# Attention's scores in another PSUM ring, and three stages of attention and retention run at later steps

## The chip, the cores and the metric

The kernel runs on one core of a Trainium2 chip, as one launch. The metric is the device time of that core in microseconds. Engines are named as in the profile: PE is TensorE's matmul (PEld its weight loads), DVE is VectorE, ACT is ScalarE, POOL is GpSimd, SP is SyncE, which here only issues DMAs.

## The reference, cut to what matters

A block of an encoder over 256 tokens of width 2048, all in float32: a half-step SwiGLU feed-forward, then two token mixers side by side, then a second half-step feed-forward and a final RMSNorm. The mixers are what the change is about:

```
q_a, k_a, v_a, q_r, k_r, v_r, g_r, gate_a, gate_r = split(rmsnorm(x) @ w_in)
att = softmax(q_a k_a^T / sqrt(128) + bias, chunk-causal) v_a             # 8 heads of 128
ret = (decay * (rotary(q_r) rotary(k_r)^T)) v_r                            # 8 heads of 128
ret = silu(g_r) * ret * rsqrt(mean(ret^2) + eps)                           # per head
x = x + (sigmoid(gate_a) * (att @ w_out_att) + sigmoid(gate_r) * (ret @ w_out_ret)) @ w_out
```

With 256 tokens there are four chunks of 64. The kernel computes retention without the recurrent state, as masked scores over all 256 tokens with the decay as a table.

## The kernel before, in words

All big products are matmuls of a 128x128 block of activations with a 128x512 block of weights. Each operand is split in a high and a low float32r part, and a product is three matmuls: high by high, low by high, high by low (`three`, L147, L148, L150). The work is a list of steps, written out in advance. A standard step takes two 128-row blocks of weights, 512 columns and both 128-token blocks: 12 matmuls. For it a weight tile is loaded by SP's queue, ACT casts it to its high part (L136) and DVE subtracts to get the low part (L137). There are four pairs of tiles for the split weights.

The order on every engine is the order in which the program is written. Step c does this:

```python
prep_upto(c + min(SPLIT_BUFS, AHEAD[0] + c // AHEAD[1]) if c else 2)
for fn in due.pop(c, []):
    fn()
steps[c].products()
state["slots"] += 1
```

So it first splits the weights of step c+3 (the fourth pair becomes free with step c-1), then runs what is due at c in the order in which it was entered with `later(n, fn)` (n steps from now), then issues its matmuls. What follows the last step of a product (its `done`) is issued behind that step's matmuls.

Entries of this list are counted here from `mixed`, the first step of the retention's queries. Entries 0 to 31 are the projections QR0, KR0, QR1, KR1 (8 entries each; 0 and 1 are halves of four heads). Entries 32 to 47 multiply the attention's result by `w_out_att`, four column blocks of 4 entries, 48 to 63 the retention's by `w_out_ret`; entry 48+j of the first block reads heads 2j and 2j+1, and the same holds for 32+j. At the end of each of the attention's blocks DVE multiplies the gate into both token blocks (`siga`, L1148).

PSUM has eight banks in three rings: `acc` and `z` of three banks each, `side` of two. A standard product holds one bank of `acc` (first token block) and one of `z` (second) for its entries. `side` serves everything short: transposes, scores, values.

Attention's head h (L952 on) is five stages at entries HEAD_AT[h] + 0, 1, 2, 4 and 6, with HEAD_AT = 3, 6, 10, 13, 17, 20, 24, 27. `scores`: two matmuls into `as` (L962, L963), DVE scales and adds the bias (L970). `powers`: ACT's exponentials. `shares`: DVE divides by the sums (L992). `transposes`: three into `apt` (L998), ACT copies them out (L1000). `values`: matmuls into `av` (L1006, L1007), then `split_out`: ACT casts to `atth` (L388), DVE subtracts to `attl` (L389).

Retention's half b is entered when its keys are done (half 0 at entry 15, half 1 at entry 31), with wait = RET_WAIT[b] = 14 and 5. Head i's `scores` (into `rs`, L1031, L1032; DVE multiplies the decay in, `rp`, L1034, L1035) run at wait + 2i, its `values` (into `ro`, one bank of `acc` and one of `z` for all four heads, L1044 to L1046) at wait + 2i + 3. `finish`, at wait + 9, squares on ACT (L1054), sums on DVE (L1056), takes the power on POOL (L385), and multiplies norm and gate in on DVE (L1062). Three entries later `ret.put` transposes both token blocks of the half, eight transposes into two tiles of the side ring (`retp`, L394), and splits them into `reth` and `retl` (L388, L389), which the products with `w_out_ret` read.

The rotated queries and keys are transposed as well (`qr0p`, `kr0p`, `qr1p`, `kr1p`, L394), at entries 10, 11, 18, 19, 26, 27, 34, 35, each entered behind the stages of attention.

Of the kernel before, what the change touches and what calls it, by code (L numbers as in the profile page):

```python
# [38 lines left out]
HALF_K = D // P // 2  # L39
LEAD = (10, 8)  # L40
MIX_LEAD = 6
RET_WAIT = (14, 5)
HELD = 6
MIX_ADDED = (0,)
MIX_AHEAD = 12
# [37 lines left out]
def block_kernel(ctx: ExitStack, tc: tile.TileContext, x, g1, w1g, w1u, w1d, gm, w_in, rel, woa, wor, wo,  # L83
# [12 lines left out]
    def act_tile(dt, name):  # L96
        return apool.tile([P, 4, SEQ], dt, tag="act", name=name)

    def acc_tile(name, tag="acc"):
        return psum.tile([P, NB], F32, tag=tag, name=name, bufs=3)  # L100

    def side_tile(name):
        return psum.tile([P, NB], F32, tag="side", name=name, bufs=2)

    def tmp_tile(name, tag="t", bufs=None):
        return tmp.tile([P, NB], F32, tag=tag, name=name, bufs=bufs)
# [9 lines left out]
    def later(n, fn):  # L116
        due.setdefault(state["step"] + n, []).append(fn)
# [263 lines left out]
    def rsqrt(dst, ssum, n, width):  # L381

        v = small.tile([P, width], F32, tag="v", name="v")
        nc.vector.tensor_scalar(v, ssum, 1.0 / n, EPS, op0=ALU.mult, op1=ALU.add)
        nc.gpsimd.tensor_tensor(dst, v, mhalf[:, :width], op=ALU.pow)  # L385

    def split_out(ps, hi, lo):
        nc.scalar.copy(hi, ps)  # L388
        nc.vector.tensor_sub(lo, ps, hi.bitcast(F32))  # L389
# [564 lines left out]
    def attention(h):  # L954
        b, i = h // 4, h % 4
        hs = slice(i * HD, (i + 1) * HD)
        sm = {}

        def scores():
            q, k = tposed["qa", b], tposed["ka", b]  # L960
            ps = side_tile(f"as{h}")
            nc.tensor.matmul(ps[:, 0:SEQ], q[:, i, P:SEQ], k[:, i, :], start=True, stop=True)  # L962
            nc.tensor.matmul(ps[:, SEQ : SEQ + P], q[:, i, 0:P], k[:, i, 0:P], start=True, stop=True)  # L963
            room = act_tile(F32, f"p{h}").rearrange("p a q -> p (a q)")
            s = room[:, : 3 * P].rearrange("p (j k) -> p j k", j=3)
            sm["room"] = room
            p3 = ps[:, : 3 * P].rearrange("p (j k) -> p j k", j=3)

            for j, bj in ((0, 1), (1, 0), (2, 0)):
                nc.vector.scalar_tensor_tensor(  # L970
                    s[:, j, :], p3[:, j, :], scale, table["bias", b][:, i, bj * P : (bj + 1) * P], op0=ALU.mult, op1=ALU.add
                )
            m = small.tile([P, NT], F32, tag="m", name="m")
            tot = small.tile([P, NT], F32, tag="l", name="l")
            for t, js in ((1, slice(0, 2)), (0, slice(2, 3))):
                nc.vector.reduce_max(m[:, t : t + 1], s[:, js, :], axis=AX.XY)
            nc.vector.tensor_scalar_mul(m, m, -1.0)
            sm["p"], sm["m"], sm["tot"] = s, m, tot


        def powers():
            s, m, tot = sm["p"], sm["m"], sm["tot"]
            for t, js in ((1, slice(0, 2)), (0, slice(2, 3))):
                nc.scalar.activation(
                    s[:, js, :], s[:, js, :], AF.Exp, bias=m[:, t : t + 1], accum_out=tot[:, t : t + 1]
                )

        def shares():
            s, tot = sm["p"], sm["tot"]
            nc.vector.reciprocal(tot, tot)  # L990
            for t, js in ((1, slice(0, 2)), (0, slice(2, 3))):
                nc.vector.tensor_scalar_mul(s[:, js, :], s[:, js, :], tot[:, t : t + 1])  # L992

        def transposes():
            ps = side_tile(f"apt{h}")

            for j, c in ((2, 0), (0, 1), (1, 2)):
                nc.tensor.transpose(ps[:, c * P : (c + 1) * P], sm["p"][:, j, :], id_sb)  # L998
            pt = sm.pop("room")[:, 3 * P : 6 * P]
            nc.scalar.copy(pt, ps[:, : 3 * P])  # L1000
            sm["pt"] = pt

        def values():
            v = nat["va", b]
            ps = side_tile(f"av{h}")
            nc.tensor.matmul(ps[:, :SEQ], v[:, 0, hs], sm["pt"][:, :SEQ], start=True, stop=False)  # L1006
            nc.tensor.matmul(ps[:, P:SEQ], v[:, 1, hs], sm["pt"][:, SEQ:], start=False, stop=True)  # L1007
            hi, lo = att.alloc(b)
            split_out(ps[:, :SEQ], hi[:, i, :], lo[:, i, :])

        return (0, scores), (1, powers), (2, shares), (4, transposes), (6, values)

    def all_attention():
        for h in range(HEADS):
            for s, stage in attention(h):
                later(HEAD_AT[h] + s, stage)

    def retention(b):

        wait = RET_WAIT[b]  # L1020
        outs = {}

        def head(i):
            h = 4 * b + i
            hs = slice(i * HD, (i + 1) * HD)
            sm = {}

            def scores():
                q, k = tposed["qr", b], tposed["kr", b]
                ps = side_tile(f"rs{h}")  # L1030
                nc.tensor.matmul(ps[:, 0:SEQ], k[:, i, 0:P], q[:, i, :], start=True, stop=True)  # L1031
                nc.tensor.matmul(ps[:, SEQ : SEQ + P], k[:, i, P:SEQ], q[:, i, P:SEQ], start=True, stop=True)  # L1032
                s = act_tile(F32, f"rp{h}").rearrange("p a q -> p (a q)")[:, : 3 * P]
                nc.vector.tensor_mul(s[:, :SEQ], ps[:, :SEQ], table["decay", b][:, i, :])  # L1034
                nc.vector.tensor_mul(s[:, SEQ:], ps[:, SEQ : SEQ + P], table["decay", b][:, i, 0:P])  # L1035
                sm["s"] = s

            def values():
                if i == 0:
                    for t in range(NT):  # L1040
                        outs[t] = acc_tile(f"ro{b}{t}", ("acc", "z")[t])
                v = nat["vr", b]
                s = sm["s"]
                nc.tensor.matmul(outs[0][:, hs], s[:, 0:P], v[:, 0, hs], start=True, stop=True)  # L1044
                nc.tensor.matmul(outs[1][:, hs], s[:, P:SEQ], v[:, 0, hs], start=True, stop=False)
                nc.tensor.matmul(outs[1][:, hs], s[:, SEQ:], v[:, 1, hs], start=False, stop=True)  # L1046

            return scores, values

        def finish():  # L1050
            srcs = []
            for t in range(NT):
                sq = tmp_tile(f"rsq{b}{t}", "gate", 2)
                nc.scalar.activation(sq, outs[t], AF.Square)  # L1054
                ms = small.tile([P, 4], F32, tag="ms", name="ms")
                nc.vector.reduce_sum(ms, sq.rearrange("p (h d) -> p h d", h=4), axis=AX.X)  # L1056
                rs = small.tile([P, 4], F32, tag="rs", name="rs")
                rsqrt(rs, ms, HD, 4)
                o = tmp_tile(f"rg{b}{t}", "qk", 4)
                for i in range(4):  # L1060
                    hs = slice(i * HD, (i + 1) * HD)
                    nc.vector.scalar_tensor_tensor(  # L1062
                        o[:, hs], outs[t][:, hs], rs[:, i : i + 1], nat["gr", b][:, t, hs], op0=ALU.mult, op1=ALU.mult
                    )
                srcs.append(o)
            later(3, lambda: [ret.put(b, t, srcs[t]) for t in range(NT)])

        for i in range(4):
            for s, stage in enumerate(head(i)):
                later(wait + 2 * i + 3 * s, stage)  # L1070
        later(wait + 2 * 4 + 1, finish)

    w_in0 = w_in[0]

# [50 lines left out]
    for b in range(2):  # L1125
        add([proj(QR + b * NB, ret_qk_done("qr", b)), proj(KR + b * NB, ret_qk_done("kr", b, lambda b=b: retention(b)))])
# [209 lines left out]
```

## Time and profile before

| what | value |
|---|---|
| runs, median (lowest to highest) | 2048.49 us (2047.64 to 2049.56), 3 runs |
| profiled execution, its own time | 2048.31 us |
| its span, first to last instruction | 2046.5 us |
| PE busy, share of the span | 2031.7 us, 99% |
| PEld, DVE, ACT, POOL busy | 1678.3, 1788.5, 1499.2, 344.8 us |
| granted clock of PE, mean | 0.999 of full speed |

The busy share of PE counts overlapping matmuls as one stretch, so a matmul that starts 0.2 us later than it could is not seen in it; the start times in a timeline tell that. The attention and retention stages lie between 1060 and 1240 us of the span. A row of a timeline is: start in us, us until the last of the group ended, engine, line, operation, output<-inputs, shapes, count, and in brackets the idle time before it with what ended it.

### The profile page before, as it was taken

What the parts mean: (1) busy time and instruction counts of PE and PEld (TensorE: products, weight loads), DVE (VectorE), ACT (ScalarE), POOL (GpSimd) and SP (SyncE); (2) the same over time, 40 slices, a digit from 0 to 9 for tenths busy, and PEclk for the clock granted to TensorE, in tenths of its full rate; (3) what the DMA queues carried; (4) which work ended last, traced back from release to release, by engine and by line L of the source; (5) the groups of instructions that cost most, each with busy time, mean ns of one, the idle gap of its engine ahead of it and who ended that gap; (6) DMA issues with size and microseconds to landing.
All of it is one profiled execution on the core that took longest, in us unless ns stands there. A gap on an engine that the chain in (4) does not pass through costs nothing.

```text
span 2046.5 us, 26320 instructions
## 1 busy us (share of the span) xinstructions
PE 2031.7 (99%) x9188; PEld 1678.3 (82%) x9188; DVE 1788.5 (87%) x1837; ACT 1499.2 (73%) x1890; POOL 344.8 (17%) x403
## 2 busy tenths in 40 slices
PE   9999999999999999999999999999999999999998
PEld 7788888888888878888888888888788888888886
DVE  7999999999998799999987667569989999989996
ACT  7788887878887777777775434556788788888785
POOL 1221122212113021211120000011112221112200
PEclk9999999999999999999999999999999999999999
DMA  8888899988878689899896645576889988889973
GB/s 289 249 248 259 254 269 278 265 242 246 264 231 264 234 228 310 272 281 286 254 321 221 212 148 197 187 240 180 269 262 269 278 248 234 267 257 268 278 206 134
DMA packets 226853, 506.33 MB, mean 247 GB/s; under 512 B 15824, under 2 KB 16576, under 8 KB 226720
## 3 DMA queue, kind: packets, MB, share of 16 engines
q1 hardware_dynamic: 154560, 297.31, 43.1%
q0 software_dynamic: 67952, 198.36, 37.1%
q10 hardware_dynamic: 4208, 8.99, 1.2%
q8 instruction: 72, 1.18, 0.2%
q14 instruction: 61, 0.50, 0.1%
HBM read 472.08 MB, written 12.06 MB: 237 GB/s over the span
## 4 chain that ended last, share of the span: by engine, by line
PE 94%; DVE 2%; DMA 2%; issue 1%; ACT 0%; POOL 0%; DVEq 0%; POOLq 0%; ACTq 0%
PE acc L150 15%; PE acc L147 15%; PE acc L148 15%; DMA z1030k<-in_ffn_w_up_dram 1%; DMA z1030x<-z1030k 1%; DVE lo L137 0%; DMA raw<-in_ffn_w_gate_dram 0%; PE z704a L150 0%; PE z425a L147 0%; PE z922a L147 0%; PE z885a L148 0%; PE z226a L147 0%; PE z190a L147 0%; PE z46a L147 0%; PE z262a L148 0%
## 5 line engine op out<-in xcount | busy, mean ns | idle before, releaser
L137 DVE TENSOR_TENSOR lo<-raw,hi 128x1024 fp32r<-128x1024 f32 x351 | 428.6, 1223 | 117.7 <-ACT hi L136 116.1
L136 ACT CAST hi<-raw 128x1024 fp32r<-128x1024 f32 x351 | 367.9, 1051 | 178.7 <-PE acc L148 133.4
L824 ACT ACTIVATE xall<-acc 128x512 f32<-128x512 f32 x160 | 94.5, 590 | 13.5 <-PE acc L150 9.7
L821 ACT ACTIVATE acc<-xall 128x512 f32<-128x512 f32 x160 | 95.9, 600 | 2.5
L147 PE MATMUL acc<-hi,mgh 128*128 128x512 f32 x128 | 50.2, 392 | 0.0
L148 PE MATMUL acc<-hi,mgl 128*128 128x512 f32 x128 | 49.8, 389 | 0.0
L150 PE MATMUL acc<-lo,mgh 128*128 128x512 f32 x128 | 35.5, 389 | 0.0
L147 PE MATMUL acc<-hi,nma01h 128*128 128x512 f32 x80 | 32.5, 407 | 0.0
L147 PE MATMUL acc<-hi,nma00h 128*128 128x512 f32 x80 | 32.3, 404 | 0.0
L148 PE MATMUL acc<-hi,nma01l 128*128 128x512 f32 x80 | 31.3, 391 | 0.0
L148 PE MATMUL acc<-hi,nma00l 128*128 128x512 f32 x80 | 31.2, 390 | 0.0
L148 PE MATMUL acc<-hi,nma11l 128*128 128x512 f32 x80 | 31.2, 390 | 0.0
L147 PE MATMUL acc<-hi,nma11h 128*128 128x512 f32 x80 | 31.2, 390 | 0.0
L147 PE MATMUL acc<-hi,nma10h 128*128 128x512 f32 x80 | 31.2, 390 | 0.0
L148 PE MATMUL acc<-hi,nma10l 128*128 128x512 f32 x80 | 31.2, 390 | 0.0
L150 PEld LDWEIGHTS acc<-lo,mgh 128*128 128x128 f32 x128 | 24.0, 188 | 5.0
L148 PEld LDWEIGHTS acc<-hi,mgl 128*128 128x128 f32 x128 | 24.0, 188 | 4.9
L147 PEld LDWEIGHTS acc<-hi,mgh 128*128 128x128 f32 x128 | 24.0, 188 | 4.9
L147 PE MATMUL acc<-hi,atth 128*128 128x512 f32 x64 | 26.2, 410 | 0.0
L147 PE MATMUL acc<-hi,reth 128*128 128x512 f32 x64 | 25.3, 395 | 0.0
L148 PE MATMUL acc<-hi,attl 128*128 128x512 f32 x64 | 25.1, 392 | 0.0
L148 PE MATMUL acc<-hi,retl 128*128 128x512 f32 x64 | 24.9, 389 | 0.0
(6884 smaller groups left out, 7265.9 us busy)
## 6 DMA issues: line engine op xcount, KB each, us to landing
raw<-in_ffn_w_down_dram SPq DMA_DIRECT2D x176, 512.0 KB, 6.8
raw<-in_w_in_dram SPq DMA_DIRECT2D x80, 512.0 KB, 5.2
raw<-in_w_out_dram SPq DMA_DIRECT2D x32, 512.0 KB, 3.7
raw<-in_ffn_w_up_dram SPq DMA_DIRECT2D x16, 512.0 KB, 4.6
raw<-in_w_out_att_dram SPq DMA_DIRECT2D x16, 512.0 KB, 4.2
raw<-in_w_out_ret_dram SPq DMA_DIRECT2D x16, 512.0 KB, 3.8
raw<-in_ffn_w_gate_dram SPq DMA_DIRECT2D x15, 512.0 KB, 4.0
z390x<-in_w_in_dram POOLq DMA_DIRECT2D x8, 512.0 KB, 9.9
```

Source lines behind the costliest of these rows:

```text
L136: nc.scalar.copy(hi, raw)
L137: nc.vector.tensor_sub(lo, raw, hi.bitcast(F32))
L147: nc.tensor.matmul(acc, ahi, whi, start=first, stop=False, **more)
L148: nc.tensor.matmul(acc, alo, whi, start=False, stop=False, **more)
L150: nc.tensor.matmul(acc, ahi, wlo, start=False, stop=last, **more)
L821: nc.scalar.activation(acc, xs[t][:, cols], AF.Copy, scale=2.0)
L824: nc.scalar.activation(xs[t][:, cols], acc, AF.Copy, scale=0.5)
```

## The change

The attention's scores get a bank of the z ring in place of one of the side ring. The attention's values run 7 entries behind the scores instead of 6: at 10, 13, 17, 20, 24, 27, 31 and 34. The retention's values run 4 entries behind their scores instead of 3, `finish` one entry later, and RET_WAIT of the second half is 6 instead of 5. So half 0 has its scores at 29, 31, 33, 35 as before, its values at 33, 35, 37, 39, `finish` at 39 and `put` at 42; half 1 has scores at 37, 39, 41, 43, values at 41, 43, 45, 47, `finish` at 47 and `put` at 50. Before they were: half 0 values at 32 to 38, `finish` 38, `put` 41; half 1 scores 36 to 42, values 39 to 45, `finish` 45, `put` 48. No instruction is added or removed.

```diff
@@ -39,7 +39,7 @@
-RET_WAIT = (14, 5)
+RET_WAIT = (14, 6)
@@ -958,7 +958,7 @@
         def scores():
             q, k = tposed["qa", b], tposed["ka", b]
-            ps = side_tile(f"as{h}")
+            ps = acc_tile(f"as{h}", "z")
@@ -1008,7 +1008,7 @@
-        return (0, scores), (1, powers), (2, shares), (4, transposes), (6, values)
+        return (0, scores), (1, powers), (2, shares), (4, transposes), (7, values)
@@ -1067,8 +1067,8 @@
         for i in range(4):
             for s, stage in enumerate(head(i)):
-                later(wait + 2 * i + 3 * s, stage)
-        later(wait + 2 * 4 + 1, finish)
+                later(wait + 2 * i + 4 * s, stage)
+        later(wait + 2 * 4 + 2, finish)
```

## Rows read from the trace of the kernel before

**Rows 1.** The page: busy time by engine, and the chain that ended last.

```profile
PE 2031.7 (99%) x9188; PEld 1678.3 (82%) x9188; DVE 1788.5 (87%) x1837; ACT 1499.2 (73%) x1890; POOL 344.8 (17%) x403
...
PE 94%; DVE 2%; DMA 2%; issue 1%; ACT 0%; POOL 0%; DVEq 0%; POOLq 0%; ACTq 0%
```

**Rows 2.** Waits of PE, whole span: us in total, times, longest.

```profile
PE as L962 <- ACT p L1000: 0.6, 1, 0.6
```

**Rows 3.** Stretches: length, busy us by engine, granted clock, DMA share, GB/s.

```profile
2038.00:2042.00 4.00, 0.01 (x1) 0.00 (x0) 2.27 (x6) 1.93 (x5) 0.55 (x1) 1.00 0.47 162
...
1060.00:1240.00 180.00, 179.22 (x880) 149.66 (x879) 125.61 (x250) 87.14 (x131) 10.89 (x17) 1.00 0.63 207
```

**Rows 4.** Timeline of PE, entry 45 and entry 48.

```profile
1213.21 0.38 PE L1044 MATMUL ro<-vr,rp 128*128 128x128 f32 x2
...
1222.09 1.03 PE L394 MATMUL retp<-id_sb,rg 128*128 128x128 f32 x8
...
1223.19 0.40 PE L148 MATMUL acc<-hi,retl 128*128 128x512 f32 x1
```

**Rows 5.** Timeline of PE, entry 10.

```profile
1090.02 0.49 PE L998 MATMUL apt<-id_sb,p 128*128 128x128 f32 x3
1091.07 0.70 PE L962 MATMUL as<-ka0back,qa0back 128*128 128x256 f32 x2 [0.57 <-ACT p L1000]
...
1091.83 0.60 PE L394 MATMUL qr0p<-id_sb,qr00r 128*128 128x128 f32 x4
```

**Rows 6.** Timeline of PE, entry 31.

```profile
1161.90 0.49 PE L998 MATMUL apt<-id_sb,p 128*128 128x128 f32 x3
1162.22 0.60 PE L1031 MATMUL rs<-qr0T,kr0T 128*128 128x256 f32 x2
```

**Rows 7.** Timeline of PE, entry 33.

```profile
1169.09 0.59 PE L1006 MATMUL av<-p,va1back 128*128 128x256 f32 x2
...
1169.74 0.60 PE L1031 MATMUL rs<-qr0T,kr0T 128*128 128x256 f32 x2
```

**Rows 8.** Timeline of ACT, entries 10 and 33.

```profile
1090.54 0.48 ACT L1000 COPY p<-apt 128x384 f32<-128x384 f32 x1
...
1169.94 0.37 ACT L388 CAST atth<-av 128x256 fp32r<-128x256 f32 x1
```

**Rows 9.** Timeline of PE, entries 38 and 41.

```profile
1187.65 0.38 PE L1044 MATMUL ro<-vr,rp 128*128 128x128 f32 x2
...
1198.57 0.38 PE L1044 MATMUL ro<-vr,rp 128*128 128x128 f32 x2
...
1199.23 1.38 PE L394 MATMUL retp<-id_sb,rg 128*128 128x128 f32 x8
```

**Rows 10.** Timeline of DVE, entries 38 to 40.

```profile
1189.17 0.68 DVE L1056 TENSOR_REDUCE ms<-rsq 128x4 f32<-128x512 f32 x1
...
1194.25 1.13 DVE L1062 SCALAR_TENSOR_TENSOR rg<-ro,rs,gr 128x128 f32<-128x128 f32 x4 [1.12 <-POOL rs L385]
...
1199.62 0.29 DVE L1035 TENSOR_TENSOR rp<-rs,decay 128x128 f32<-128x128 f32 x1
```

**Rows 11.** Timeline of DVE, entries 45 to 48.

```profile
1215.17 0.68 DVE L1056 TENSOR_REDUCE ms<-rsq 128x4 f32<-128x512 f32 x1
...
1221.26 2.35 DVE L137 TENSOR_TENSOR lo<-raw,hi 128x1024 fp32r<-128x1024 f32 x2
1223.53 1.28 DVE L1148 TENSOR_TENSOR siga<-acc,siga 128x512 f32<-128x512 f32 x2
1224.72 1.22 DVE L137 TENSOR_TENSOR lo<-raw,hi 128x1024 fp32r<-128x1024 f32 x1
1225.86 1.28 DVE L389 TENSOR_TENSOR retl<-retp,reth 128x512 fp32r<-128x512 f32 x2
```

**Rows 12.** Timeline of DVE, entry 10.

```profile
1094.17 0.69 DVE L970 SCALAR_TENSOR_TENSOR p<-as,bias 128x128 f32<-128x128 f32 x3
```

## The prediction

> **What bounds the kernel now.** I read the page first: the matmul engine PE is busy for 99% of the span, and the chain that ended last is 94% PE [rows 1]. Next the waits of PE over the whole span: only one of them lies in the attention and retention part, a score matmul waiting for ScalarE (ACT) [rows 2]. The table by stretch puts that part at 1060 to 1240 us: PE busy 179.22 of 180 us at full clock, VectorE (DVE) 125.61, ACT 87.14 [rows 3]. So PE is the bound here, the others run at its pace, and a change of order can pay only by taking away PE's waits. There is under 1 us of these. Last I read the timelines of PE, ACT and DVE around the entries that the diff touches, to see which waits go and which come.
>
> Entries are counted from the first entry of the retention's queries (entry 0, `mixed`). Entry n of the run does three things in this order: it splits the weights of entry n+3 (ACT casts, DVE subtracts), runs what is due, and issues its own matmuls. An entry without inserts takes 2.74 us: entries 45 to 47, with one `ro` group of 0.66 us, go from 1213.21 to 1222.09, (8.88 - 0.66) / 3 [rows 4]. A wait on PE is not made good later: those 36 matmuls already follow each other every 0.228 us.
>
> The weight loads are busy for 149.66 of the 180 us, 83% [rows 3]. The Trainium skill, page "Perfetto Trace Analysis", section "Identifying the Most-Contended Engine", calls matmul busy time a poor measure of headroom and takes this share instead. By it 30 us of the stretch would be slack, new waits could vanish in it, and the sum would stay at 2048.3; by the even spacing of the matmuls it would be 2052.0.
>
> **Scores in the z ring.** The instructions are the same; only the bank differs. In the old order entry 10 issues the transposes of head 1 and then the scores of head 2 out of the two-bank side ring. The scores start 1.05 us after the transposes [rows 5], where the same two groups stand 0.32 us apart at entry 31 [rows 6], and the wait is for the copy of the transposed shares, ACT L1000 [rows 2]. So the ring had handed out the bank just transposed into, the one that came free first. With the scores in z this wait of 0.73 us goes. In z I followed the banks by hand on that rule: each score tile and each projection finds one freed several entries earlier (KR0 gets that of head 0's scores, QR1 that of head 2's), so these moves cost nothing. That is hidden by the third bank; without it KR0 would wait for ACT's reading of QR0, behind six matmuls of its first token block.
>
> **Attention's values an entry later.** They now run at entries 10, 13, 17, 20, 24, 27, 31 and 34, in front of other groups that use the side ring. Where two groups of one entry use it there is a bank for each. Where three do, the third waits. That is so at entries 10 and 31.
>
> At entry 10 (start S): values 0.65 us (the spacing of `av` and the next group [rows 7]), transposes 0.32, scores 0.65 (the same two shapes), then the first transposes of QR0, at S+1.62. Their bank is that of head 1's transposed shares. ACT casts the values at S+0.85 (1169.94 against 1169.09) for 0.37, copies the shares at S+1.22 for 0.48 [rows 7, 8], and the bank is free at S+1.70, with 0.05 for the signal 1.75. Wait 0.13; net of the old one -0.60.
>
> At entry 31 no scores stand between. Values, transposes of head 7, then retention's second scores, at S+0.97, with the bank again free at S+1.75: +0.78. In the old order these two groups went through at once [rows 6]. Bounds: 0, and 1.1 if the bank is that of the values, which also needs the weights' subtract and the values' own.
>
> Head 7's values at entry 34 are first read in entry 35, behind most of an entry's matmuls; their subtract waits for one split, so nothing. The tiles with the shares stay one entry longer, which can delay by 2.74 us the loads on POOL's queue that reuse them (decay, gates). The gates are loaded 12 entries before they are multiplied, which hides it; past that, it would be the whole excess. On SP's queue nothing moves.
>
> **Retention's values an entry later, its second half another.** First half: values at 33 to 39, end (`finish`) at 39 instead of 38. Second half: scores at 37 to 43, values at 41 to 47, `finish` at 47 instead of 45. What `finish` makes is transposed into the operand `ret` three entries later (`put`): now at 42 and 50 instead of 41 and 48. The outputs' matmuls read the second half from entry 50 on, so that `put` now stands directly in front of its first reader. DVE runs in order, so its subtract (`retl`) is queued behind all that DVE has.
>
> Entry 42 (`put` of half 0). In the old order the second group of transposes waited for DVE's reading of the scores before (L1035): the eight take 1.38 us at 1199.23 and 1.03 at 1222.09, so 0.35 [rows 4, 9]. From the entry of `finish` (1187.65) to the end of that reading (1199.91) are 12.26 us of DVE [rows 9, 10]; the new order has the same DVE work there, in another sequence. PE comes to these transposes earlier, for the group `ro` in front of them (1198.57 to 1199.23, 0.66 [rows 9]) is gone: 11.58 - 0.66 = 10.92 after the start of entry 39, the second four at 11.3. Wait 12.31 - 11.3 = 1.0, net +0.65. Part may show already at entry 41, where the second half's outputs may get the z bank that `finish` reads until 7.73 (1195.38 [rows 10]), while PE comes there at some 7.0; what is lost there is not lost again at 42. Bounds 0 and 1.4.
>
> Entry 50 (`put` of half 1). Old: from the first reduction of `finish` (1215.17) DVE does `finish`, two weight splits, two products of the gates, a third split and the first `retl`, which ends near 1226.50: 11.33 us [rows 11]. The new order has the same between 47 and 50: `finish`, two products, splits of 51, 52 and 53, `retl`. The reduction begins 1.52 us (entry 38) or 1.96 us (entry 45) after its entry starts [rows 4, 9 to 11]; I take 1.52, since the entry before 47, like that before 38, is a middle one of its group, where the weights' slot comes free earlier. So `retl` ends 12.85 after the start of entry 47, 12.90 with the signal. PE needs it at 8.88 (start of 50) + 1.10 (from the transposes to the first matmul with a low part, 1222.09 to 1223.19 [rows 4]) = 9.98. Wait 2.92. Bounds: 0, were the three splits (3.4 us) done before, which DVE's order excludes as far as I see; 4.0 with 1.96 and both `retl` waited for.
>
> **Sum.** -0.60 + 0.78 + 0.65 + 2.92 = +3.75 us on the profiled execution's 2048.31 (its span 2046.5 and 1.8 around it), which is 0.18 under the median of the runs. That is 2052.1; I say 2052.0. 0.2% of this kernel, about what a measurement can tell from no change, is 4.1 us, so up to 2052.6.
>
> **Rivals.**
> (a) The wait at 50 hardly shows, because DVE is less behind than at entry 45. For it: DVE is busy for 125.61 of 180 us [rows 3]. Against: from `finish` on it has no gap but those for POOL's powers. Sum +0.83: 2049.1.
> (b) Waits go and none come: -0.73, 2047.6. Against it: three groups, two banks.
> (c) Slower: at entry 10 QR0's transposes get the bank of head 0's values, whose subtract is queued on DVE right in front of the scores' first scaling, now at 1094.17 [rows 12]. PE would come there at 1089.37 (0.65 before 1090.02) + 1.62 = 1091.0 and wait 3.2: 2055.2. It decides once the copy of the shares is later than that subtract. Against it: the ring gave the ACT bank in the old order.
> (d) Slower: the wait at 50 brings the clock down to 1.2 GHz. In the 4 us after the last matmul, with PE idle, the granted clock was still 1.00 [rows 3], longer than 2.92. One entry at half speed costs 2.74: 2054.7. The Trainium skill, page "TensorE: Matmul & The Clock Gate", section "What's actually happening", has the array's clock gated by how busy it has lately been; by that rule (d) could happen, and the row speaks against it here.
>
> **How the numbers follow.** The forecast has 0.63, its own range 2050.6 to 2053.2; the bounds of the terms put 0.22 of that above 2052.6 and 0.41 below. (a) 0.12, (b) 0.05, (c) 0.10, (d) 0.05; something not seen 0.05, of it 0.03 a gain and 0.02 a loss. Within 0.2%: 0.41 + 0.12 + 0.05 = 0.58. Slower: 0.22 + 0.10 + 0.05 + 0.02 = 0.39. Faster: 0.03, since PE has no 4 us of waits here to give back. From 2048.9 to 2054.8 leaves out (b), (c) and what was not seen: 0.8.
>
> **What would show it.** Right: no wait of the score matmuls for L1000; a wait of some 0.8 us before the scores `rs` of entry 31; about 1 us at entry 41 or 42 for DVE L1062 or L1035; one near 2.9 us of a matmul at L148 with `retl` for DVE L389. Wrong: no wait for L389 (then (a)); a wait of `qr0p` for L389 (then (c)); a granted clock under 1.00 near 1235 us (then (d)).

## The result, and the profile after

| what | before | after |
|---|---|---|
| median of 12 runs each (lowest to highest) | 2048.11 us (2047.09 to 2050.23) | 2052.98 us (2051.84 to 2055.22) |
| ratio of the medians, 95% interval | | 1.0024 (1.0017 to 1.0031) |
| profiled execution, its own time (span) | 2048.31 us (2046.5) | 2054.64 us (2052.9) |

The changed kernel is slower by 4.9 us, 0.24%. The forecast was 2052.0, the range 2048.9 to 2054.8. The loss lies beside the bound of 0.2%, and the interval, 3.5 to 6.3 us, reaches to both sides of it. The profiled execution is 1.7 us above the median of its kernel; the last paragraph of this section says where that lies.

The page of the changed kernel first: busy time by engine, and the chain that ended last.

```profile
PE 2034.8 (99%) x9188; PEld 1680.3 (82%) x9188; DVE 1789.1 (87%) x1837; ACT 1498.9 (73%) x1890; POOL 344.8 (17%) x403
...
PE 39%; DVE 0%; issue 0%; ACT 0%; DVEq 0%; POOLq 0%; POOL 0%
```

Against [rows 1] the instructions are the same in number, and PE is busy for 3.1 us more with them, which slower matmuls would give. The chain can be followed back over 39% of the span only, the part behind attention and retention, so it does not say what happened there. The waits do. This is the view of PE's waits from 1060 to 1250 us (us in total, times, longest):

```profile
PE acc L148 <- DVE retl L389: 2.3, 1, 2.3
PE ro L1045 <- DVE rg L1062: 0.7, 1, 0.7
PE rs L1031 <- ACT p L1000: 0.6, 1, 0.6
PE acc L147 <- ACT reth L388: 0.2, 1, 0.2
```

The one wait of [rows 2] is gone, and four have come. A listed wait is only the idle part of what a late start costs, so the costs are read from starts, in PE's timeline. From top to bottom: entry 10, entry 31, entry 41, the `put` at 42, the start of entry 47, and entry 50.

```profile
1089.72 0.49 PE L998 MATMUL apt<-id_sb,p 128*128 128x128 f32 x3
1090.05 0.60 PE L962 MATMUL as<-ka0back,qa0back 128*128 128x256 f32 x2
...
1090.78 0.66 PE L394 MATMUL qr0p<-id_sb,qr00r 128*128 128x128 f32 x4
...
1160.75 0.49 PE L998 MATMUL apt<-id_sb,p 128*128 128x128 f32 x3
1161.81 0.70 PE L1031 MATMUL rs<-qr0T,kr0T 128*128 128x256 f32 x2 [0.57 <-ACT p L1000]
...
1196.79 0.38 PE L1044 MATMUL ro<-vr,rp 128*128 128x128 f32 x2
1197.87 0.46 PE L1045 MATMUL ro<-vr,rp 128*128 128x128 f32 x2 [0.70 <-DVE rg L1062]
...
1198.39 0.60 PE L1031 MATMUL rs<-qr1T,kr1T 128*128 128x256 f32 x2
...
1201.80 1.16 PE L394 MATMUL retp<-id_sb,rg 128*128 128x128 f32 x8
...
1218.92 0.38 PE L1044 MATMUL ro<-vr,rp 128*128 128x128 f32 x2
...
1227.81 1.04 PE L394 MATMUL retp<-id_sb,rg 128*128 128x128 f32 x8
...
1231.87 0.50 PE L148 MATMUL acc<-hi,retl 128*128 128x512 f32 x1 [2.29 <-DVE retl L389]
...
1232.67 0.59 PE L147 MATMUL acc<-hi,reth 128*128 128x512 f32 x1
1233.06 0.63 PE L148 MATMUL acc<-hi,retl 128*128 128x512 f32 x1
...
1236.04 0.44 PE L147 MATMUL acc<-hi,reth 128*128 128x512 f32 x1
```

Entry 10: the scores follow the transposes after 0.33 us, where it was 1.05 [rows 5]. `qr0p` follows them after 0.73 instead of the 0.65 of these shapes, so 0.08 is left (experiment 5 says what it is). Entry 31: 1.06 between transposes and scores instead of 0.32 [rows 6]. Entry 41: from the first `ro` to the next group 1.60 instead of 0.66 [rows 9]. Entry 42: the eight transposes take 1.16 instead of 1.38 [rows 9], near the 1.03 of an undisturbed group [rows 4]. Entry 50: the first matmul with a low part starts 4.06 after the transposes instead of 1.10 [rows 4]. And from 1232.67 on the matmuls stand 0.4 apart.

What PE waits for at entry 50 is seen in DVE's timeline, entries 47 to 50:

```profile
1220.44 0.68 DVE L1056 TENSOR_REDUCE ms<-rsq 128x4 f32<-128x512 f32 x1
...
1225.49 1.13 DVE L1062 SCALAR_TENSOR_TENSOR rg<-ro,rs,gr 128x128 f32<-128x128 f32 x4 [1.12 <-POOL rs L385]
1226.53 1.28 DVE L1148 TENSOR_TENSOR siga<-acc,siga 128x512 f32<-128x512 f32 x2
1227.73 3.49 DVE L137 TENSOR_TENSOR lo<-raw,hi 128x1024 fp32r<-128x1024 f32 x3
1231.13 1.28 DVE L389 TENSOR_TENSOR retl<-retp,reth 128x512 fp32r<-128x512 f32 x2
```

It is the sequence of [rows 11], only that all three splits now stand together behind the gates' products. From 1226.53 on DVE runs without a gap, and `retl` is last in its queue. PE's transposes are through at 1228.85, while DVE still has about two of the three splits ahead.

What PE did behind the wait is seen in the table by stretch (columns as in [rows 3]; the granted clock is the third number from the end):

```profile
1229.30:1232.70 3.40, 1.11 (x5) 0.70 (x5) 3.11 (x4) 0.22 (x1) 0.00 (x0) 1.00 0.72 217
1232.70:1236.10 3.40, 3.40 (x10) 2.63 (x9) 0.00 (x0) 1.04 (x1) 0.00 (x0) 0.50 0.71 249
1236.10:1239.50 3.40, 3.40 (x16) 2.80 (x15) 3.02 (x4) 0.91 (x1) 0.00 (x0) 1.00 0.19 59
```

In the first stretch, that of the wait, the clock is still 1.00. In the next it is 0.50, which is 1.2 GHz; PE is busy throughout and gets 10 matmuls done where the stretch behind has 16. Then the clock is full again. So the wait costs a second time.

If the start of the same matmul is compared in both traces, step by step, the changed kernel is 0.28 us ahead at the start of entry 3, 3.33 behind just after the wait of entry 50, and 4.91 behind after the slow stretch: +3.6 for the order, +1.6 for the clock, +5.2 for this part. The profiles of experiments 10 and 11, of the same changed kernel, give +5.2 as well. Behind 1250 us the order is as before; there the profiled execution loses another 1.4, most of it in waits for weight splits near 1450 us. In the profiles of the experiments this tail lies between -0.6 and +1.6 with no relation to what was changed. It is scatter between executions, and most of why the profiled execution lies above the median.

### The profile page after: what moved, and what is told of

The parts are those of the page before. It is cut to its first block, busy times and chain, and to the rows that moved or that the text cites. A ratio compares the mean times of both kernels' runs of the same rounds, so it can differ in the third digit from the quotient of the medians.

```text
span 2052.9 us, 26316 instructions
## 1 busy us (share of the span) xinstructions
PE 2034.8 (99%) x9188; PEld 1680.3 (82%) x9188; DVE 1789.1 (87%) x1837; ACT 1498.9 (73%) x1890; POOL 344.8 (17%) x403
## 5 line engine op out<-in xcount | busy, mean ns | idle before, releaser
L147 PE MATMUL acc<-hi,mgh 128*128 128x512 f32 x128 | 50.2, 392 | 0.0
L147 PE MATMUL acc<-hi,nma01h 128*128 128x512 f32 x80 | 32.4, 405 | 0.0
L147 PE MATMUL acc<-hi,nma00h 128*128 128x512 f32 x80 | 32.1, 401 | 0.0
L147 PE MATMUL acc<-hi,nma10h 128*128 128x512 f32 x80 | 31.2, 390 | 0.0
L147 PE MATMUL acc<-hi,nma11h 128*128 128x512 f32 x80 | 31.2, 390 | 0.0
L147 PEld LDWEIGHTS acc<-hi,mgh 128*128 128x128 f32 x128 | 24.0, 188 | 4.9
L147 PE MATMUL acc<-hi,reth 128*128 128x512 f32 x64 | 25.8, 403 | 0.2 <-ACT reth L388 0.2
L147 PE MATMUL acc<-hi,atth 128*128 128x512 f32 x64 | 26.0, 406 | 0.0
```

Source lines behind the costliest of these rows:

```text
L147: nc.tensor.matmul(acc, ahi, whi, start=first, stop=False, **more)
```

## The experiments

The theory: PE's order costs 3.6 us, nearly all of it the wait at entry 50, and the half-speed stretch behind that wait adds 1.6. The rivals: the lower clock has nothing to do with the wait; the loss comes from the attention's part; or the wait is not one for DVE's queue. Each table line is one kernel. The runs of the kernel before on the same chip had medians of 2048.45 us (1 to 8) and 2048.75 us (9 to 11). The longest wait is that of PE between 1060 and 1250 us, and the clock is that of the stretch of some 3.4 us behind it, both in the one profiled execution.

| kernel | median us, runs | ratio (95%) | longest wait us | clock behind it |
|---|---|---|---|---|
| changed | 2052.98, 12 | 1.0024 (1.0017 to 1.0031) | 2.29 | 0.50 |
| 1 changed, wait filled with matmuls | 2052.49, 11 | 1.0022 (1.0013 to 1.0030) | filled | 1.00 |
| 2 retention's part alone | 2052.88, 11 | 1.0021 (1.0013 to 1.0030) | 2.29 | 1.00 |
| 3 attention's part alone | 2048.10, 11 | 0.9999 (0.9990 to 1.0008) | 0.57 | 1.00 |
| 4 changed, gates' products later | 2050.56, 11 | 1.0010 (1.0002 to 1.0019) | 1.09 | 1.00 |
| 5 scores in z alone | 2047.51, 11 | 0.9995 (0.9986 to 1.0004) | none listed | |
| 6 values at 7, scores in side | 2056.19, 5 | 1.0039 (1.0026 to 1.0051) | 2.36 | 0.50 |
| 7 scores in z, first `put` an entry later | 2048.52, 11 | 1.0000 (0.9991 to 1.0009) | 0.92 | 1.00 |
| 8 changed, one more DVE subtract | 2055.45, 5 | 1.0034 (1.0021 to 1.0048) | 3.42 | 0.50 |
| 9 changed, RET_WAIT 5 again | 2050.14, 11 | 1.0009 (0.9999 to 1.0018) | 1.42 | 1.00 |
| 10, 11 changed, once more | 2052.96 and 2053.16 | | 2.28, 2.28 | 0.50, 0.50 |

**1. The wait filled.** Between the transposes of entry 50 and the products, PE gets 12 matmuls whose result nobody reads. They depend on nothing late.

```diff
-            later(3, lambda: [ret.put(b, t, srcs[t]) for t in range(NT)])
+            def put():
+                for t in range(NT):
+                    ret.put(b, t, srcs[t])
+                if b == 1:
+                    bank = acc_tile("fill", "z")
+                    x = ret.hi[0].rearrange("p a q -> p (a q)")
+                    for _ in range(12):
+                        nc.tensor.matmul(bank, x[:, 0:P], x[:, 0:NB], start=True, stop=True)
+            later(3, put)
```

> The changed kernel with twelve 512-column matmuls more (into a free bank of the z ring, read by nobody) between the transposes and the products of entry 50, so that PE works through the wait of 2.96 us for the low part instead of standing still. Twelve at 0.228 us are 2.74 us, which fit into the wait. Theory 1 (the idle time at entry 50 lowers the clock, and this costs 1.6 us behind the wait): the granted clock stays at 1.00 behind entry 50, the first matmul with a low part starts at the same distance from the start of entry 47 (12.95 us), and the kernel is about 1.6 us faster than the changed one where that one loses its clock, so +3.3 us on the kernel before. Theory 2 (the clock fell by accident in the profiled execution, or for the whole kernel's sake): a stretch at 0.50 shows here as well, or the time is that of the changed kernel, +4.9 us. If the matmuls cost time by themselves, over +5.

PE's timeline of this kernel at entry 50, then its table by stretch:

```profile
1228.45 1.03 PE L394 MATMUL retp<-id_sb,rg 128*128 128x128 f32 x8
1229.24 2.98 PE L1074 MATMUL fill<-reth 128*128 128x512 f32 x12
...
1232.52 0.50 PE L148 MATMUL acc<-hi,retl 128*128 128x512 f32 x1
```

```profile
1229.60:1232.80 3.20, 3.12 (x14) 2.30 (x13) 3.20 (x4) 0.56 (x2) 0.00 (x0) 1.00 0.59 186
1232.80:1236.20 3.40, 3.40 (x16) 2.75 (x16) 0.92 (x2) 1.05 (x1) 0.00 (x0) 1.00 0.87 275
```

The low part is no earlier (4.07 after the transposes), but the clock stays at 1.00 and 16 matmuls go through where the changed kernel had 10. In the step-by-step comparison this kernel loses 3.66 over the same entries, as the order alone does, and 0.06 behind. That fits a clock that falls because PE stands idle in the wait. One profile does not show it, since experiment 2 has the wait and keeps the clock; the clocks of all runs, behind experiment 11, say more. In the times the gain is 0.5 us (2052.49 against 2052.98) or, by the differences to each one's kernel before, 0.8; the intervals overlap, so the times alone do not show the 1.6.

**2. Retention's part alone.** The kernel before with the two last hunks of the diff and RET_WAIT (14, 6).

> The kernel before with the retention's part of the change alone (values 4 entries behind, second half an entry later); attention as before. Theory 1: the loss comes from the transposes in front of their first reader at entry 50: a wait of 2.9 us for the low part, 0.75 to 1.0 us at entries 41 and 42 (less the 0.35 of before), and 1.6 us where the clock falls: +3.5 us without the clock, +5.1 with it. The old wait of 0.7 us of the score matmuls at entry 10 stays. Theory 2 (the loss comes from the attention's three groups on two banks): at most +1 us, and no wait for the low part.

Its time is +4.4 us, within the intervals that of the whole change. From its timeline of PE and its table by stretch:

```profile
1231.44 0.50 PE L148 MATMUL acc<-hi,retl 128*128 128x512 f32 x1 [2.29 <-DVE retl L389]
```

```profile
1231.70:1235.10 3.40, 3.40 (x16) 2.77 (x16) 0.94 (x2) 1.05 (x1) 0.00 (x0) 1.00 0.78 257
```

The wait is the same to 0.01 us, and yet the clock did not fall in this execution. Its step-by-step loss is +3.7, the order alone, and its own time, 2050.67, is the lowest of the 11 runs of this kernel. That suits a clock that falls in some executions and not in others, which the clocks of all runs bear out (behind experiment 11).

**3. Attention's part alone.** The kernel before with the scores in z and `(7, values)`.

> The kernel before with the attention's part alone (scores in the z ring, values 7 entries behind); retention as before. Theory 1: the wait of 0.7 us at entry 10 goes and one of 0.75 us at entry 31 comes, so 0.0 to +0.2 us, which no timing tells from no change; no wait for a low part of the retention, clock at 1.00. Theory 2 (the loss comes from here): +4 us or more.

It is -0.35 us, no difference that can be measured. The one wait left in the view is that of `rs` for L1000, 0.57 us, in place of the old one for the same copy; its scores stand 1.06 us behind the transposes, as in the changed kernel. The loss is retention's.

**4. The gates' products later.** In the changed kernel the two products `siga` of the attention's last block (1.28 us of DVE) are put off by four entries, so that they no longer stand ahead of `retl`. The sum is the same.

```diff
-        def branch_a_done(acc, sig=sig):
-            for t in range(NT):
-                nc.vector.tensor_mul(sig["a"][:, t, :], acc[t], sig["a"][:, t, :])
+        def branch_a_done(acc, sig=sig, b=b):
+            def go():
+                for t in range(NT):
+                    nc.vector.tensor_mul(sig["a"][:, t, :], acc[t], sig["a"][:, t, :])
+            if b == D // NB - 1:
+                later(4, go)
+            else:
+                go()
```

> The changed kernel, with the last two products of the attention's gates (DVE, 1.2 us, at the end of entry 47) put four entries later, so behind the low part of entry 50 in DVE's order. Theory 1 (the wait is DVE's queue from the end of the retention's norm on): the wait at entry 50 shrinks by 1.2 us, from 2.96 to 1.75; if the clock stays up after the shorter wait, the kernel is 1.2 + 1.6 us faster than the changed one with its clock lost: +2.1 us on the kernel before; if it falls again, +3.7. Theory 2 (the wait is for the transposes and casts themselves, whatever DVE has before): it stays near 2.9 us.

PE's timeline of this kernel:

```profile
1230.23 0.50 PE L148 MATMUL acc<-hi,retl 128*128 128x512 f32 x1 [1.09 <-DVE retl L389]
...
1231.03 0.39 PE L147 MATMUL acc<-hi,reth 128*128 128x512 f32 x1
...
1232.84 0.39 PE L147 MATMUL acc<-hi,reth 128*128 128x512 f32 x1
```

The wait is 1.20 us shorter, the length of DVE's two products in the chain (1226.53 to 1227.73 after). The kernel comes out at +2.1 us, 2.8 less than the changed one, which is the 1.20 and the 1.6 of the clock, here at 1.00; the intervals, 0.4 to 3.9 and 3.5 to 6.3, just overlap. The two last rows are the same matmuls as those at 1232.67 and 1236.04 of the changed kernel; they are 1.81 us apart here and 3.37 there. So the slow stretch costs 1.56 us. And what makes PE wait is DVE's queue: taking one item out of it takes that item's time off the wait.

**5. Scores in z alone.** One line of the diff.

> The kernel before with the scores in the z ring alone. Theory 1 (the third bank takes away the one wait of the score matmuls and brings none): no wait of a score matmul at entry 10, all other starts of PE up to entry 60 as before, -0.7 us or -0.8, which no timing tells from no change. Rival (the z ring is short of banks for the projections): a wait of a first matmul of KR0, QR1 or KR1 on ACT's reading, +0.5 us or more each.

PE's timeline of this kernel, entry 10:

```profile
1090.29 0.49 PE L998 MATMUL apt<-id_sb,p 128*128 128x128 f32 x3
1090.62 0.60 PE L962 MATMUL as<-ka0back,qa0back 128*128 128x256 f32 x2
...
1091.35 0.66 PE L394 MATMUL qr0p<-id_sb,qr00r 128*128 128x128 f32 x4
```

The view of PE's waits from 1060 to 1250 us is empty. The trace is 0.7 us shorter there; `qr0p` follows the scores after 0.73 here too, 0.05 after the end of ACT's copy of the shares, as in the changed kernel. So the 0.08 of entry 10 is not the price of the values' move. With only two groups in the side ring at this entry the second still gets the bank of the first: DVE reads the other one, with the values of entry 9, until 1091.40. The times (2047.51 against 2048.45) do not tell this kernel from the one before. It is the lowest median of all, but not a version that is shown to beat the kernel before.

**6. Values at 7 with the scores in the side ring.** The third line of the diff without the second.

> The kernel before with the attention's values 7 entries behind the scores, the scores left in the side ring. Theory 1 (three groups of one entry on two banks make the third wait): at entries 10, 17 and 24 the scores wait 0.75 us for ACT's copy of the shares in front of them, at 10 the queries' transposes 2 us more for the values' subtract, at 27 the queries' transposes 1.9 us for the same, at 31 as in the changed kernel 0.75: in all 7.2 us, less the 0.8 of before: +6 us. Rival (these waits come from ACT's pace and not from the banks): the same waits as with the scores in z, 0.75 at entry 31 alone, +0.1 us.

From the view of PE's waits and the table by stretch of this kernel:

```profile
PE as L962 <- ACT p L1000: 2.5, 3, 1.4
PE qr0p L394 <- DVE attl L389: 2.4, 1, 2.4
PE qr1p L394 <- DVE attl L389: 0.8, 1, 0.8
```

```profile
1091.00:1095.00 4.00, 1.22 (x7) 0.98 (x8) 4.00 (x12) 0.37 (x1) 0.53 (x1) 1.00 0.59 190
...
1095.60:1098.90 3.30, 3.30 (x9) 2.52 (x9) 0.33 (x2) 0.75 (x2) 0.00 (x0) 0.50 0.50 173
```

Slower by 7.7 us: without the bank in z three groups of one entry, at entry 10 four, share two banks, and `qr0p` waits 2.36 us for the subtract of the values. This is what rival (c) described, in the kernel to which it would have applied. Behind that wait, at another place of the kernel and for another reader, the clock fell again; 0.57 us of waiting stand close before it, and PE is busy for 1.22 of the 4 us of the first stretch.

**7. Scores in z, the first half's `put` an entry later.** The kernel before with `later(4 - b, ...)` in place of `later(3, ...)` and the scores in z: a try at taking away the wait of the old entry 41 too.

> The kernel before with the scores in the z ring and the put of retention's half 0 one entry later (42 instead of 41; its first reader is entry 48). Half 1 as before. Theory 1: takes away the two waits of PE that the attention and retention part had, 0.73 us at entry 10 and 0.35 at entry 41: -1.1 us, 0.05%, less than a timing tells. Rival (put at 42 meets another group of the side ring): a wait of 0.5 us or more there, no gain.

PE's timeline of this kernel, entry 42:

```profile
1203.57 0.66 PE L394 MATMUL retp<-id_sb,rg 128*128 128x128 f32 x4 [0.92 <-DVE rp L1035]
```

No gain: entry 42 has the scores of a retention head in the side ring as well, and the second four transposes wait for the bank that DVE reads at L1035. The move went past one conflict into another of the same kind.

**8. One more DVE subtract ahead of `retl`.** A 128x1024 subtract whose result nobody reads, in the changed kernel:

```diff
-            later(3, lambda: [ret.put(b, t, srcs[t]) for t in range(NT)])
+            def put():
+                if b == 1:
+                    more = act_tile(F32, "more")
+                    nc.vector.tensor_sub(more, ret.lo[0].bitcast(F32), ret.hi[0].bitcast(F32))
+                for t in range(NT):
+                    ret.put(b, t, srcs[t])
+            later(3, put)
```

> The changed kernel with one more subtraction of 128x1024 on DVE (1.14 us, its result is not used) in front of the low parts of entry 50. Theory 1 (the wait is DVE's queue): it grows by 1.14 us, from 2.96 to 4.1. Theory 2 (the clock falls behind a wait of some 3 us in most executions, not in all; behind 1.75 us it did not): behind 4.1 us it falls in nearly all, so +3.7 + 1.1 + 1.6 = +6.4 us on the kernel before. If the wait were for PE's own transposes, it would stay at 2.96 and the time at +4.9.

PE's timeline and the table by stretch of this kernel:

```profile
1233.50 0.79 PE L148 MATMUL acc<-hi,retl 128*128 128x512 f32 x1 [3.42 <-DVE retl L389]
```

```profile
1232.80:1236.10 3.30, 2.60 (x6) 2.12 (x7) 1.24 (x3) 0.00 (x0) 0.00 (x0) 0.50 0.80 263
1236.20:1239.40 3.20, 3.20 (x9) 2.49 (x8) 0.75 (x1) 1.04 (x1) 0.00 (x0) 0.50 0.10 36
1239.60:1243.00 3.40, 3.40 (x16) 2.81 (x15) 2.72 (x5) 1.05 (x1) 0.00 (x0) 1.00 0.48 150
```

The wait grew by 1.13 us, and the clock stayed low for two stretches instead of one; in all +7.0 us. DVE's queue sets the wait in this direction too, and behind the longer wait the low clock lasted twice as long.

**9. RET_WAIT of the second half back at 5.** The changed kernel with its first line undone: the second half's `put` at entry 49 instead of 50, an entry ahead of its first reader.

> The changed kernel with the second half's start as before (RET_WAIT 5): scores at 36 to 42, values at 40 to 46, finish at 46, put at 49, one entry ahead of its first reader. Theory 1 (DVE's queue against the distance to the reader): the low part is ready 12.9 us after the start of entry 46 and wanted at 12.6, so a wait of 0.3 us in place of 2.96, and no fall of the clock; but the values of entry 40 come one entry behind the first half's finish, so a product or a value at entry 40 waits about 1.6 us for DVE's reading of the first half's outputs: in all +2.2 us on the kernel before. Rival (the distance to the reader doesn't matter, the three stages later do): +3.7 us or more.

From the view of PE's waits:

```profile
PE acc L147 <- DVE rg L1062: 1.4, 1, 1.4
PE rs L1031 <- ACT p L1000: 0.6, 1, 0.6
PE retp L394 <- DVE rp L1035: 0.3, 1, 0.3
```

No wait for `retl` is listed any more. The wait for `finish` of the first half doubled, from 0.70 to 1.42: the second half's outputs take their banks an entry sooner, and now it is a matmul of the standard product of entry 40 (L147) that waits. The trace says +2.1 us; the median says +1.4 (interval -0.2 to +3.7).

**10 and 11. The changed kernel once more**, for its clock.

> The changed kernel once more, for one profile. The wait for the low part at entry 50 is 2.96 us again. The clock behind it: theory (it falls in most executions, by chance) 0.50 for 3.4 us here with some 7 in 10; if it falls in this one and in the next, it is likely no matter of chance; if in neither, it is rare and explains little of the difference.

> The changed kernel a third time, for one profile, as the run before.

The table by stretch, of one and then of the other:

```profile
1232.70:1236.00 3.30, 3.30 (x9) 2.58 (x8) 0.00 (x0) 1.04 (x1) 0.00 (x0) 0.50 0.78 258
```

```profile
1231.70:1235.00 3.30, 3.30 (x9) 2.54 (x8) 0.23 (x1) 0.42 (x1) 0.00 (x0) 0.50 0.82 269
```

The fall came in three of three profiles of the changed kernel.

**The clock of every run.** For every run its mean granted clock is on record, to three places. 3.4 us at half the clock take 0.0008 off the mean of 2050 us. All five profiles with a fall in this part have 0.998 or 0.997, and of the eight without one only that of experiment 4 has 0.998, the others 0.999. So 0.999 tells of no fall, and 0.998 leaves it open.

| kernels | runs at 0.999 |
|---|---|
| longest wait 1.42 us or less: experiments 3, 4, 5, 7, 9 and the kernel before beside the experiments | 104 of 124 |
| wait of 2.29 us: changed | 2 of 14 |
| wait of 2.29 us: experiment 2 | 4 of 11 |
| wait filled: experiment 1 | 6 of 11 |
| waits of 2.36 and 3.42 us: experiments 6 and 8 | 1 of 10 |

So the fall goes with the long wait, in most runs and not in all: it is no accident of the profiled executions. In experiment 2 the four runs at 0.999 have a mean of 2051.85 us and the other seven 2053.38, a difference of 1.5, near the 1.6 of the traces. Experiment 1 lies between, on 11 runs; that filling the wait keeps the clock up every time is not shown.

## Why the prediction was right, and where it failed

**The bound.** That PE is the bound here and that waits on it are not made good later held: +3.6 in the starts is still there after the part, and the matmuls that follow at full clock are as closely spaced as before. The Trainium skill, page "Perfetto Trace Analysis", section "Identifying the Most-Contended Engine", judges headroom by the share of weight loads, beside that of the peak arithmetic. The prediction read from it that new waits could vanish in the 17% in which no weights are loaded; the trace disagrees: of 3.78 us of waits 3.61 were still there at a later matmul.

**The terms of the order.**

| term | predicted us | measured in starts us |
|---|---|---|
| entry 10, old wait gone, new one | -0.73 and +0.13 | -0.72 and +0.08 (not from the values' move) |
| entry 31 | +0.78 | +0.74 (1.06 less 0.32) |
| entries 41 and 42 | +0.65 | +0.94 - 0.22 = +0.72 |
| entry 50 | +2.92 | +2.96 (4.06 less 1.10) |
| sum | +3.75 | +3.78 (3.61 as the lag of a later matmul) |

The banks went as the prediction had followed them by hand: at 10 and 31 the third group of the entry got the bank that ACT's copy frees first. Only its rule that two groups of one entry find a bank each fails at entry 10, by experiment 5, for 0.08 us. The wait for `finish` showed at entry 41, not at 42, as the second of the two places that were named. The waiting time at 50 came out of DVE's queue: the reduction began 1.52 us after the start of entry 47, the value taken, and `retl` was ready 12.95 after that start, for 12.90. Experiments 4 and 8 shortened and lengthened that queue, and the wait followed.

**The step that failed is that of rival (d)**: "In the 4 us after the last matmul, with PE idle, the granted clock was still 1.00 [rows 3], longer than 2.92." From that row the clock was taken to outlast the wait, and (d) got 0.05. The sign that the prediction named for (d), a clock under 1.00 near 1235 us, showed. The row is right, but the same view of the kernel before has the stretch right behind it, which [rows 3] leaves out:

```profile
2042.70:2046.50 3.80, 0.00 (x0) 0.00 (x0) 0.00 (x0) 0.00 (x0) 0.00 (x0) 0.50 0.49 167
```

So the trace of before did have a fall behind PE's idle time, only a late one: PE's last matmul ended at 2038.01. In the changed kernel it is late too, 1.00 in the stretch of the wait and 0.50 in the next, when PE is at work again. That the clock holds while PE stands idle does not tell that it holds behind the wait. It fell in three of three profiles of the changed kernel, behind an idle time of 2.29 us; experiment 2, where the same wait left the clock alone, shows that one execution can go either way. The Trainium skill, page "TensorE: Matmul & The Clock Gate", section "What's actually happening", has the clock gated by PE's recent activity; by that rule the fall could come, and the prediction let the row decide against it. The traces of the changed kernel and of experiment 1 agree with the rule (0.50 behind the idle wait, 1.00 behind the filled one); that of experiment 2, 1.00 behind the idle wait, does not show it.

**The price of (d)** was too high: the prediction took one entry at half speed, 2.74 us, where the slow stretch of 3.4 us holds about eight matmuls and cost 1.56. Order and clock together are 3.6 + 1.6 = 5.2 in the traces, and the median of the runs says 4.9. So the time lies 1.0 above the forecast mainly for one reason, which was named and given too small a chance: by the terms as predicted and the clock as measured the forecast would have been 2048.3 + 3.75 + 1.6 = 2053.7, 0.7 above the median. That 2052.98 still lies in the forecast's own range, 2050.6 to 2053.2, is luck in part: that range was made for the terms of the order, at full clock. The whole range, up to 2054.8, took (d) in.

**The other rivals.** (a): the wait at 50 did show. (b): waits came. (c): `qr0p` did not wait for L389, since the copy of the shares was done at 1090.73 and the subtract came later; experiment 6 shows that it is what happens when the scores stay in the side ring.

**What stays open.** What decides whether the clock falls behind a wait of 2.29 us, since one profile of four with that wait shows no fall, and at least 6 of its 25 runs had none. And how much of the 4.9 us of the median is the clock's: the traces say 1.6 in those executions where it fell, experiment 4's time bears that out as a sum with the wait, and experiment 1's time alone does not resolve it.

## What to carry to other kernels

Before a producer is moved next to its first reader, list what its in-order engine has queued ahead of it at that moment: here what DVE did in the 12.9 us from the start of entry 47 set the wait, and it could be counted to 0.05 us from the trace of before. For every ring of banks count the groups that one step asks for: a third or fourth group on two banks waited 0.6 to 2.4 us in these kernels, and where one of the groups moved to another ring (entry 10, experiment 6 against 3) the wait went. Price a new wait of two or three microseconds on the matmul engine as possibly paid twice, once as idle time and once at a lower clock behind it.

## What the runs showed of the hardware

The granted clock of PE fell to 0.50 behind waits of 2.28 and 2.29 us (three profiles of the changed kernel), 2.36 us (experiment 6, with 0.57 close before) and 3.42 us (experiment 8), though PE had been busy for nearly all of the time before. It did not fall behind the same 2.29 us in experiment 2, nor behind 1.09 and 1.42 us in experiments 4 and 9, nor with the wait filled in experiment 1. By the clocks of all runs it falls behind such a wait in most executions, not in all. At half speed the 128x512 matmuls followed each other every 0.43 us instead of 0.23, for about 3.4 us, which cost 1.56 us; behind 3.42 us of waiting it lasted 6.8 us. At the end of the kernel before the clock was still 1.00 through four idle microseconds [rows 3] and 0.50 from 2042.70 us on.
